# A hybrid encoder layer: weight loads, value splits, output projection and mixture in a new order

## The chip, the cores and the metric

The kernel runs on one core of a Trainium2 chip. The metric is the device time of one execution in microseconds; for the kernel before it is the median of three runs. The engines are TensorE (PE), VectorE (DVE), ScalarE (ACT), GpSimd (POOL) and SyncE (SP, which issues DMAs).

## The reference, cut to what matters

Both batches (1024 tokens, "a"; 512 tokens, "b") go through the same layer with the same weights, in f32:

```python
h = rms_norm(x, pre_w)
cols = jnp.einsum('bsd,dc->bsc', h, w_in)          # 1024 -> q|k, v, o, z, gates, attention q,k,v, z, merge gates
y_m = mlstm_mixer(...) * silu(m_z)                 # 4 heads x 256, both directions, chunks of 128
y_a = dilated_attention(a_qkv, rel_table) * silu(a_z)   # 3 groups x 8 heads x 64, mixed by softmax denominators
merged = g[:, :, 0] * (y_m @ w_pm) + g[:, :, 1] * (y_a @ w_pa)
out = merged @ w_out
return x + rms_norm(out, post_w)
```

## The kernel before, in words

**Precision.** Nearly every product is three matmuls: each operand is split into a rounded high part (ACT copy) and the rest as a low part (DVE or POOL subtraction), and `mm3` (L174 to L179) adds high x high, high x low and low x high. A split must be ready before the product's first matmul (L177) and its low part before the second or third.

**Part one** (to about 1030 us) projects batch a with a Strassen-like scheme: 7 products instead of 8 for a 2x2 block form. `combos` makes the seven combinations of the input, H. `value_group` (L347) makes the value columns in 4 groups; a group has 7 products (m1, m2, m6, m7, m5, m4, m3), each of 4 token tiles x 4 k x 3 = 48 matmuls of 322 columns. Its splits (L362 ACT, L363 DVE) use two buffers (vhi and vlo, `bufs=2`) in turn, in the order in which they are traced: m1's, then s2 (for m6), then w12 (for m2), and so on. PSUM has 8 banks, and a product takes 4. Evictions are DVE adds (such as L409 and L436), high/low splits into vz (L387, L388; three buffers) and stores (L389, L392). Each group loads its weights (va, vb) and makes sums of them on POOL (L343 to L345, vsum). `lanes` is a chain of small gate computations on ACT and DVE with a few PE transposes; its steps are advanced one by one between the products of groups 1 and 2. Then 38 calls of `unit_pair` (L439) make the other columns, two units of 128 columns at a time: two loads (L445), splits (L453, L454), POOL sums, 7 products of 12 matmuls of 512 columns.

In part one PE's order is the program's. The orders of ACT, DVE, POOL and SP are chosen when the kernel is compiled, by a scheduler that prefers what stands earlier in the program among what it takes to be ready; `high_priority` puts an instruction ahead of others. On the chip each engine then works strictly in its order.

**Part two** (from about 1030 us) runs the mLSTM of a, the attention of a, the mLSTM of b, the attention of b and the rest, in rounds (`mlstm` L788, `attend` L1142). In every round `fill` puts in dense work: a list of units (projections of batch b, then for each block of 512 tokens the two branch projections w_pm and w_pa and the output projection w_out), cut into steps of 3 matmuls of 512 columns or 6 of 256. `STEPS` (L1410) sets how many steps fall into each stage. Here the orders of PE and SP are both the program's.

`Fill.load` (L124) and `load_w` (L221) bring the weights: `load_w` issues the DMA into one of two raw buffers (L229) and traces the split (L230 ACT, L231 DVE) into one of three ring buffers, five after the third stage. `ready` counts the weights split, `taken` those in use, `base` the first still held; `ahead` is how many may be split ahead (2, later 3).

`final` (L1359) is the output projection of a block: for each half u of the columns it takes four weights at once and runs 4 token tiles t one after the other, 8 k-steps of three matmuls each, in one of two PSUM banks. A tile is closed by a square with a sum (L1388 ACT), and, for the first half, a product with the post-norm weights (L1390 DVE), for the second the norm (L1394 to L1397), the residual from tile xo (loaded at L1384, two buffers) and the sum (L1400); the result is stored at the next tick (L193) or, for the last tile, at once (L1404).

`combine` (L1201) mixes the three dilation groups of a token tile: `load(t+1)`, `mix(t)` (some 15 DVE instructions, L1219 to L1239), a yield, `turn(t-1)` (PE transposes L1244, DVE product L1246), a yield. The mixture of a runs beside the rounds of the mLSTM of b, one step a round; that of b beside the last fill steps. `split` (L1272) then fetches the rows (tile ymr, L1281) for the branch projections.

`tick` (L195) issues stores that have come due and some of the queued loads (L214); `spread` (L205) sets how many a tick, so that the loads for the next attention unit are spread over the rounds of the present one; `need` issues what is still queued.

Of the kernel before, what the change touches and what calls it, by code (L numbers as in the profile page):

```python
# [112 lines left out]
class Fill:  # L113
# [3 lines left out]
    def __init__(self, net, units):  # L117
        self.net, self.units, self.gen = net, list(units), None
        self.srcs = [x for u in self.units for x in u.srcs]
        self.ready, self.taken, self.base, self.ahead = [], 0, 0, 2  # L120
        self.rate = self.due = 0.0
        self.done = 0

    def load(self):  # L124
        while len(self.ready) < min(self.base + len(self.net.wsplit), self.taken + self.ahead, len(self.srcs)):
            self.ready.append(self.net.load_w(*self.srcs[len(self.ready)]))

    def weights(self, first=True):

        if first:  # L130
            self.base = self.taken
        self.taken += 1
        self.load()
        return self.ready[self.taken - 1]

# [25 lines left out]
class Net:  # L161
# [59 lines left out]
    def load_w(self, src, kt=KT, cols=P):  # L221

        nc = self.nc
        n = kt * cols
        raw = self.wraw.pop(0)
        hi, lo = self.wsplit.pop(0)
        self.wraw.append(raw)
        self.wsplit.append((hi, lo))
        nc.sync.dma_start(raw[:, :n], src)  # L229
# [117 lines left out]
    def value_group(self, g, T, H, sb, us, co, ps):  # L347

        nc = self.nc
        N = 4 * VW  # L350
        wa = sb.tile([P, 2, N], F32, name="va", bufs=1)
# [7 lines left out]
        def split(x):  # L359
            hi = sb.tile([P, N], F32R, name="vhi", bufs=2)  # L360
            lo = sb.tile([P, N], F32R, name="vlo", bufs=2)
            nc.scalar.activation(hi, x, AF.Copy)  # L362
            nc.vector.tensor_sub(lo, x, hi.bitcast(F32))  # L363
# [11 lines left out]
        def out(t, blk, jc, c):  # L375
# [7 lines left out]
            if a0 < a1:  # L383
# [5 lines left out]
                nc.sync.dma_start(T.vs[:, r, a0 - 16:a1 - 16].rearrange("a t c -> t a c"), z[:, :, :w].bitcast(F32))  # L389
            a0 = max(lo, 16 + D)  # L390
            if a0 < hi:
                nc.sync.dma_start(T.av[r, a0 - 16 - D:hi - 16 - D], c[:, a0 - c0:])  # L392
# [3 lines left out]
        m1 = product(B11, split(wa[:, 0]))  # L396
# [31 lines left out]
        yield  # L428
        m4 = product(T4, split(wb[:, 1]))
# [4 lines left out]
        m3 = product(B22, split(s[:, 1]))  # L434
        for t in range(4):
# [3 lines left out]
    def unit_pair(self, ua, ub, H, sb, cp, ps):  # L439

        nc = self.nc
        ws = []
        for u in (ua, ub):
            w = sb.tile([P, 2, BLK], F32, name="pw_raw", bufs=4)
            last = nc.sync.dma_start(w, self.a["w_in"][u].rearrange("p (a c) -> p a c", a=2))  # L445
            ws.append(w)
        wa, wb = ws

        def split(x):
            n = x.shape[1]  # L450
            hl = sb.tile([P, 2, 2, BLK], F32R, name="phl", bufs=4)
            hi, lo = hl[:, 0], hl[:, 1]
            nc.scalar.activation(hi[:, :n], x, AF.Copy)  # L453
            nc.vector.tensor_sub(lo[:, :n], x, hi[:, :n].bitcast(F32))  # L454
            return [(hi[:, i].rearrange("p (k c) -> p k c", c=P), lo[:, i].rearrange("p (k c) -> p k c", c=P))
                    for i in range(n)]
# [7 lines left out]
        a11, a12 = split(wa)  # L464
        s = sb.tile([P, 2, BLK], F32, name="psum_w", bufs=2)
        self.sums(wa, wb, s)
        s1, s2 = split(s)
        nc.gpsimd.tensor_sub(s[:, 1], wa[:, 1], s[:, 1])
        s3, a22 = split(wb)
# [3 lines left out]
        u2 = sb.tile([P, BLK], F32, name="pu2", bufs=2)  # L473
# [6 lines left out]
        u3 = sb.tile([P, BLK], F32, name="pu3", bufs=1)  # L480
# [6 lines left out]
        s4, = split(s[:, 1:2])  # L487
        m3 = product(B22, s4)
        nc.vector.tensor_add(q[0][1], u2, m3)
        return c, last  # L490
# [651 lines left out]
    def attend(self, T, fill, steps, first, banks, outs, after=None, beside=None, at=()):  # L1142
# [5 lines left out]
        with ExitStack() as st:  # L1148
# [52 lines left out]
    def combine(self, T, bank, cs, ys, sb):  # L1201
# [50 lines left out]
        for t in range(T.n):  # L1252
# [33 lines left out]
    def along(self, units, make, every):  # L1286
# [3 lines left out]
        def wrap(u, last):  # L1290
            def go(weights):
# [7 lines left out]
                if last:  # L1299
                    for _ in got["g"]:  # L1300
                        pass
# [57 lines left out]
    def final(self, T, b):  # L1359
# [4 lines left out]
        def make(weights):  # L1364
# [6 lines left out]
            for u in range(2):  # L1371
                c = slice(u * BLK, (u + 1) * BLK)
                w = [[x.rearrange("p (k c) -> p k c", c=BLK) for x in weights(kp == 0)] for kp in range(4)]
                for t in range(4):
                    r0 = b * BLK + t * P
                    ts = slice(t * P, (t + 1) * P)
                    p = self.ps_d.tile([P, BLK], F32, name="dense")
                    for k in range(KT):
                        wk = w[k // 2]
                        hi, lo = m[k // 4]  # L1380
                        self.mm3(p, (hi[:, k % 4, ts], lo[:, k % 4, ts]), (wk[0][:, k % 2], wk[1][:, k % 2]), k == 0, k == KT - 1)
                        if k == 3 and u == 1:
                            xt = xo[t] = sb.tile([P, D], F32, name="xo", bufs=2)
                            nc.sync.dma_start(xt, T.x[r0:r0 + P])  # L1384
                        if k < KT - 1:
                            yield
                    jk = sb.tile([P, BLK], F32, name="mg", bufs=2)
                    nc.scalar.activation(jk, p, AF.Square, accum_out=ss[:, t, u:u + 1])  # L1388
                    if u == 0:
                        nc.vector.tensor_mul(o[:, t], p, pw[:, c])  # L1390
# [250 lines left out]
```

## Time and profile before

| what | value |
|---|---|
| runs of the kernel before | 2473.7, 2474.91, 2484.87 us; median 2474.91 |
| the profiled execution | 2470.32 us, of which the span from the first to the last instruction is 2468.4 |
| mean granted TensorE clock | 0.969 |
| DVE, ACT, POOL busy | 1515.6, 1126.4, 742.9 us |
| DMA | 419.86 MB, 170 GB/s on the mean |

A busy PE is one with at least one matmul in flight. Idle time before an instruction is put down to what released it. The granted clock is 1 or 0.5 at any moment; a mean below 1 over a stretch says what part of it ran at half speed.

### The profile page before, as it was taken

What the parts mean: (1) busy time and instruction counts of PE and PEld (TensorE: products, weight loads), DVE (VectorE), ACT (ScalarE), POOL (GpSimd) and SP (SyncE); (2) the same over time, 40 slices, a digit from 0 to 9 for tenths busy, and PEclk for the clock granted to TensorE, in tenths of its full rate; (3) what the DMA queues carried; (4) which work ended last, traced back from release to release, by engine and by line L of the source; (5) the groups of instructions that cost most, each with busy time, mean ns of one, the idle gap of its engine ahead of it and who ended that gap; (6) DMA issues with size and microseconds to landing.
All of it is one profiled execution on the core that took longest, in us unless ns stands there. A gap on an engine that the chain in (4) does not pass through costs nothing. (4 is left out here: it accounts for less than half of the span.)

```text
span 2468.4 us, 36244 instructions
## 1 busy us (share of the span) xinstructions
PE 2300.6 (93%) x12486; PEld 1994.0 (81%) x12486; DVE 1515.6 (61%) x2957; ACT 1126.4 (46%) x2389; POOL 742.9 (30%) x924
## 2 busy tenths in 40 slices
PE   4989899999999999999999999989988989989878
PEld 4888888888888888798998798978877878777766
DVE  7664467679986555467777554545698534445464
ACT  5331134444444333366765465556555444434322
POOL 5212133243332233145555200010355231324022
PEclk8999999999999999999999999999999989999999
DMA  3342244553222242555567678875776575585653
GB/s 146 106 113 88 101 185 184 197 188 118 102 100 89 94 145 103 195 201 194 167 213 208 173 210 226 223 199 168 220 226 200 169 249 183 181 249 177 205 182 127
DMA packets 251582, 419.86 MB, mean 170 GB/s; under 512 B 24872, under 2 KB 149992, under 8 KB 251400
## 3 DMA queue, kind: packets, MB, share of 16 engines
q1 hardware_dynamic: 247944, 404.98, 51.8%
q10 hardware_dynamic: 3456, 12.58, 1.3%
q8 instruction: 99, 1.62, 0.3%
q14 instruction: 83, 0.68, 0.1%
HBM read 297.48 MB, written 128.39 MB: 173 GB/s over the span
## 5 line engine op out<-in xcount | busy, mean ns | idle before, releaser
L177 PE MATMUL d<-Hh,phl 128*128 128x512 f32 x1064 | 415.3, 390 | 7.2 <-ACT phl L453 7.2
L179 PE MATMUL d<-Hh,phl 128*128 128x512 f32 x1064 | 415.5, 390 | 1.8 <-DVE phl L454 1.8
L178 PE MATMUL d<-Hl,phl 128*128 128x512 f32 x1064 | 415.0, 390 | 0.0
L231 DVE TENSOR_TENSOR wl<-wraw,wh 128x1024 fp32r<-128x1024 f32 x130 | 166.2, 1279 | 203.7 <-ACT wh L230 203.2
L177 PE MATMUL dense<-H,wh 128*128 128x512 f32 x672 | 281.1, 418 | 10.8 <-ACT wh L230 6.2
L179 PE MATMUL dense<-H,wl 128*128 128x512 f32 x672 | 267.6, 398 | 0.0
L178 PE MATMUL dense<-H,wh 128*128 128x512 f32 x672 | 267.6, 398 | 0.0
L177 PEld LDWEIGHTS d<-Hh,phl 128*128 128x128 f32 x1064 | 200.4, 188 | 49.1 <-ACT phl L453 7.5
L179 PEld LDWEIGHTS d<-Hh,phl 128*128 128x128 f32 x1064 | 200.4, 188 | 45.5 <-DVE phl L454 4.2
L178 PEld LDWEIGHTS d<-Hl,phl 128*128 128x128 f32 x1064 | 200.4, 188 | 41.7
L230 ACT ACTIVATE wh<-wraw 128x1024 fp32r<-128x1024 f32 x130 | 137.6, 1058 | 192.5 <-DMA wraw<-w_in 76.0
L1113 ACT ACTIVATE ls<-ls,nm 128x256 f32<-128x256 f32 (+1 forms) x288 | 129.9, 452 | 106.7 <-DVE nm L1111 89.6
L453 ACT ACTIVATE phl<-pw_raw 128x1024 fp32r<-128x1024 f32 x76 | 80.5, 1060 | 170.9 <-PE d L179 120.9
L179 PEld LDWEIGHTS dense<-H,wl 128*128 128x128 f32 x672 | 128.8, 192 | 30.8 <-DVE wl L231 1.4
L177 PEld LDWEIGHTS dense<-H,wh 128*128 128x128 f32 x672 | 129.4, 193 | 27.5 <-ACT wh L230 6.6
L178 PE MATMUL d<-vlo,Hh 128*128 128x322 f32 x448 | 144.3, 322 | 7.7 <-DVE vlo L363 7.7
L177 PE MATMUL d<-vhi,Hh 128*128 128x322 f32 x448 | 145.4, 325 | 6.4 <-ACT vhi L362 6.4
L453 ACT ACTIVATE phl<-psum_w 128x1024 fp32r<-128x1024 f32 x76 | 64.3, 846 | 190.6 <-PE d L179 153.7
L1109 DVE CUSTOM_DVE_ANT_0 ls<-lg,bias 128x256 f32<-128x256 f32 (+1 forms) x288 | 93.2, 360 | 91.3 <-PE lg L1097 40.7
L343 POOL TENSOR_TENSOR psum_w<-pw_raw 128x512 f32<-128x512 f32 x38 | 60.5, 1592 | 279.5 <-DMA pw_raw<-w_in 260.6
L179 PE MATMUL d<-vhi,Hl 128*128 128x322 f32 x448 | 143.4, 320 | 0.0
L178 PEld LDWEIGHTS dense<-H,wh 128*128 128x128 f32 x672 | 129.5, 193 | 15.6
(497 smaller groups left out, 5805.7 us busy)
## 6 DMA issues: line engine op xcount, KB each, us to landing
pw_raw<-w_in SPq DMA_DIRECT2D x76, 512.0 KB
wraw<-w_in SPq DMA_DIRECT2D x76, 512.0 KB
aqk_a<-pwk SPq DMA_DIRECT2D x48, 512.0 KB
aqk_b<-sw SPq DMA_DIRECT2D x48, 256.0 KB
wraw<-w_pm SPq DMA_DIRECT2D x24, 512.0 KB
wraw<-w_out SPq DMA_DIRECT2D x24, 512.0 KB
wraw<-w_v SPq DMA_DIRECT2D x18, 512.0 KB
erep<-erow SPq DMA_DIRECT2D x16, 512.0 KB
```

Source lines behind the costliest of these rows:

```text
L177: nc.tensor.matmul(out, lh, rh, start=start, stop=False)
L178: nc.tensor.matmul(out, lh, rl, start=False, stop=False)
L179: nc.tensor.matmul(out, ll, rh, start=False, stop=stop)
L230: self.splits = (nc.scalar.activation(hi[:, :n], raw[:, :n], AF.Copy), nc.vector.tensor_sub(lo[:, :n], raw[:, :n], hi[:, :n].bitcast(F32)))
L231: nc.vector.tensor_sub(lo[:, :n], raw[:, :n], hi[:, :n].bitcast(F32)))
L343: nc.gpsimd.tensor_add(s[:, 0], wb[:, 0], wb[:, 1])
L453: nc.scalar.activation(hi[:, :n], x, AF.Copy)
L1109: nc.vector.tensor_tensor_reduce(out=ls[:, hh], in0=ts["lg"][hh], in1=bt[:, hh], scale=1.0, scalar=NEG, op0=OP.add, op1=OP.max, accum_out= ...
L1113: nc.scalar.activation(ls[:, hh], ls[:, hh], AF.Exp, bias=nm[:, hh:hh + 1], accum_out=ot[:, 128 + hh:129 + hh])
```

## The change

Seven edits, in the order of the program:

1. **Weights of fill units.** The load and the split are parted (`fetch`, `split_w`). Each time a weight is split, the load of the one after it is issued too.
2. **Value groups.** The first split's buffers are taken ahead of the group's loads; splits are traced with high priority; w12 is split before s2; the last product's evictions come after a yield of their own; `lanes` advances at every second step.
3. **Start of the pairs.** The last value group is stopped before its last evictions; the value tiles are given back; the first pair's loads and its first two splits are traced; only then come the evictions (behind the second split on DVE) and eight stores (`late`, behind the loads on SP). The tiles u move to the other side of SBUF, so that the pair's tiles lie over the value weights.
4. **Pairs.** Loads and splits of every pair have high priority; the four split buffers become two kinds of two.
5. **Both attentions.** All loads for unit 1 are issued in the first round after they are queued.
6. **Output projection.** Two token tiles overlap: slot by slot, k-steps 4 to 7 of one tile alternate with k-steps 0 to 3 of the next, two at a time, and after each pair of k-steps of a half's last tile `release` gives a weight's buffer back and loads on.
7. **Mixture.** Three steps a tile instead of two, with the transposes two yields after the mixture of the next tile; the last attention has 300 fill steps instead of 330, and the mixture of b 86 instead of 50.

The core of the diff:

```diff
     def load(self):
         while len(self.ready) < min(self.base + len(self.net.wsplit), self.taken + self.ahead, len(self.srcs)):
-            self.ready.append(self.net.load_w(*self.srcs[len(self.ready)]))
+            self.fetch(len(self.ready) + 1)
+            self.ready.append(self.net.split_w(*self.raws[len(self.ready)]))
+            self.fetch(len(self.ready) + 1)
+
+    def fetch(self, n):
+        while len(self.raws) < min(n, len(self.srcs)):
+            self.raws.append(self.net.load_w(*self.srcs[len(self.raws)]))
...
+    def release(self):
+        self.base += 1
+        self.load()
...
     def load_w(self, src, kt=KT, cols=P):
         raw = self.wraw.pop(0)
+        self.wraw.append(raw)
+        self.nc.sync.dma_start(raw[:, :kt * cols], src)
+        return raw, kt * cols
+
+    def split_w(self, raw, n):
         hi, lo = self.wsplit.pop(0)
...
-        def split(x):
-            hi = sb.tile([P, N], F32R, name="vhi", bufs=2)
-            lo = sb.tile([P, N], F32R, name="vlo", bufs=2)
-            nc.scalar.activation(hi, x, AF.Copy)
-            nc.vector.tensor_sub(lo, x, hi.bitcast(F32))
+        def split(x, at=None):
+            hi, lo = at or place()
+            with self.tc.high_priority():
+                nc.scalar.activation(hi, x, AF.Copy)
+                nc.vector.tensor_sub(lo, x, hi.bitcast(F32))
...
+        w12 = split(wa[:, 1])
         s2 = split(s[:, 1])
-        w12 = split(wa[:, 1])
...
+        if late is not None:
+            store = lambda *x: late.append(x)
         m4 = product(T4, split(wb[:, 1]))
...
         m3 = product(B22, split(s[:, 1]))
+        yield
         for t in range(4):
...
+    def pair_split(self, x, hl):
+        n = x.shape[1]
+        hi, lo = hl[:, 0], hl[:, 1]
+        with self.tc.high_priority():
+            self.nc.scalar.activation(hi[:, :n], x, AF.Copy)
+            self.split_end = self.nc.vector.tensor_sub(lo[:, :n], x, hi[:, :n].bitcast(F32))
...
+    def pair_weights(self, ua, ub, sb):
...
+            with self.tc.high_priority():
+                last = self.nc.sync.dma_start(w, self.a["w_in"][u].rearrange("p (a c) -> p a c", a=2))
...
-                            self.spread(T.n - 1)
+                            self.spread(T.n - 1 if i else 1)
...
                 mix(t)
             yield
+            yield
             if t > 0:
                 turn(t - 1, az[t - 1])
             yield
+        yield
         yield
         turn(T.n - 1, az[T.n - 1])
...
+            w, p = {}, {}
+            for slot in range(2 * 8 + 2):
+                for i in (slot // 2 - 1, slot // 2):
+                    u, t = divmod(i, 4)
+                    if not 0 <= i < 8:
+                        continue
+                    kp = slot - 2 * i
+                    if t == 0:
+                        w[u, kp] = [x.rearrange("p (k c) -> p k c", c=BLK) for x in weights(u == kp == 0)]
+                    if kp == 0:
+                        p[i] = self.ps_d.tile([P, BLK], F32, name="dense")
...
+                    for k in (2 * kp, 2 * kp + 1):
...
+                        if k == KT - 1:
+                            close(u, t, c, p.pop(i))
+                        if t == 3 and k % 2 == 1:
+                            weights.__self__.release()
...
-STEPS = (310, 232, 194, 330, 50)
+STEPS = (310, 232, 194, 300, 86)
...
-                        for _ in values[g]:
-                            next(lanes, None)
+                        for j, _ in enumerate(values[g]):
+                            if j % 2 == 0:
+                                next(lanes, None)
...
-                for _ in values[3]:
-                    pass
-            with ExitStack() as s2:
-                sb = N.pool(s2, "pairs", 1, "left")
+                for _ in range(7):
+                    next(values[3])
+            with ExitStack() as s4:
+                sb = N.pool(s4, "pairs", 1, "left")
+                coming = N.pair_weights(U_AQ, U_AQ + 1, sb)
+                with tc.issue_after(N.split_end.ins):
+                    for _ in values[3]:
+                        pass
+                for x in late:
+                    with tc.issue_after(coming[1].ins):
+                        nc.sync.dma_start(*x)
+                s2.close()
...
-            fill.ahead = 3
+            fill.ahead = 4
...
-                fill.stage(STEPS[4], 2 * B.n + 4)
+                fill.stage(STEPS[4], 3 * B.n + 6)
```

More of the change, by code (lines that the diff above doesn't have):

```diff
@@ L119, in __init__ @@
         self.srcs = [x for u in self.units for x in u.srcs]
-        self.ready, self.taken, self.base, self.ahead = [], 0, 0, 2
+        self.raws, self.ready, self.taken, self.base, self.ahead = [], [], 0, 0, 2
         self.rate = self.due = 0.0
@@ L345, in sums, with value_group @@
         nc.gpsimd.tensor_sub(wb[:, 0], wa[:, 0], wb[:, 0])
-    def value_group(self, g, T, H, sb, us, co, ps):
+    def value_group(self, g, T, H, sb, us, co, ps, late=None):
         nc = self.nc
+        store = nc.sync.dma_start
         N = 4 * VW
+        place = lambda: [sb.tile([P, N], F32R, name=x, bufs=2) for x in ("vhi", "vlo")]
+        first = place()
         wa = sb.tile([P, 2, N], F32, name="va", bufs=1)
@@ L462, in product @@
             return p
[L464 to L467, printed above, removed]
         nc.gpsimd.tensor_sub(s[:, 1], wa[:, 1], s[:, 1])
-        s3, a22 = split(wb)
+        s3, a22 = split(wb, places[0])
         c = [cp.tile([P, 2 + 2 * BLK], F32, name="c") for _ in range(2)]
@@ L486, in unit_pair @@
         nc.vector.tensor_add(q[1][0], u3, m4)
-        s4, = split(s[:, 1:2])
+        s4, = split(s[:, 1:2], places[1])
         m3 = product(B22, s4)
         nc.vector.tensor_add(q[0][1], u2, m3)
-        return c, last
+        return c
     def conv_unit(self, u, T, raw, w):
@@ L1385, in make @@
[L1385 to L1390, printed above, removed]
-                        yield
-                        continue
-                    o1 = sb.tile([P, BLK], F32, name="mg", bufs=2)
-                    nc.vector.tensor_add(ss[:, t, 4:5], ss[:, t, 0:1], ss[:, t, 1:2])
@@ L1445, in co @@
                     return opened[0]
-                values = [N.value_group(g, A, H, vw, us, co, ps) for g in range(4)]
+                values = [N.value_group(g, A, H, vw, us, co, ps, late if g == 3 else None) for g in range(4)]
                 N.small(N.const)
```

105 lines of the change are left out of this document (55 added, 50 removed).

## The prediction

> **What bounds the kernel now.** I read the page first. TensorE (PE) is busy for 2300.6 of 2468.4 us; no other engine passes 61%. What can be won is PE's idle time (167.8 us) and the time in which PE ran at a reduced clock.
>
> ```profile
> span 2468.4 us, 36244 instructions
> ...
> PE 2300.6 (93%) x12486; PEld 1994.0 (81%) x12486; DVE 1515.6 (61%) x2957; ACT 1126.4 (46%) x2389; POOL 742.9 (30%) x924
> ...
> PE   4989899999999999999999999989988989989878
> PEclk8999999999999999999999999999999989999999
> ```
>
> The last row is the clock in tenths: the slices under 9 lie where PE's row dips. Next I read the waits of PE (what waited, for whom: us, times, longest).
>
> ```profile
> PE dense L177 <- ACT wh L230: 14.0, 3, 6.8
> PE lg L1097 <- DMA V1a<-aqk_b: 8.9, 2, 7.3
> PE d L178 <- DVE vlo L363: 7.7, 5, 2.6
> PE d L177 <- ACT phl L453: 7.2, 1, 7.2
> PE tp L1244 <- DVE Q L1239: 6.9, 1, 6.9
> PE a L1244 <- DVE wd L1226: 6.5, 1, 6.5
> PE d L177 <- ACT vhi L362: 6.4, 5, 1.9
> ```
>
> Each of these lines is a place that the change edits. Last, I took the busy times of the stretches around them (start:end, length, PE, PEld, DVE, ACT, POOL, PEclk, DMA share, GB/s).
>
> ```profile
> 107.86:132.69 24.83, 18.52 (x98) 17.71 (x98) 13.21 (x19) 8.42 (x19) 3.07 (x1) 0.79 0.54 161
> 174.43:196.77 22.34, 17.44 (x96) 16.72 (x97) 10.16 (x15) 5.93 (x12) 3.10 (x1) 0.85 0.59 156
> 196.77:221.60 24.83, 24.83 (x170) 24.83 (x169) 14.07 (x22) 5.13 (x4) 0.33 (x1) 1.00 0.28 90
> 232.52:252.55 20.03, 17.22 (x99) 15.89 (x99) 5.55 (x7) 4.21 (x6) 2.96 (x1) 0.91 0.10 35
> 288.29:305.00 16.71, 9.47 (x29) 7.11 (x29) 5.14 (x4) 3.72 (x5) 9.13 (x6) 0.69 0.49 166
> 1800.00:1850.00 50.00, 40.43 (x215) 34.14 (x214) 46.19 (x133) 27.87 (x64) 23.93 (x43) 0.93 0.73 222
> 1995.00:2020.00 25.00, 16.07 (x72) 13.14 (x72) 9.00 (x16) 11.78 (x24) 9.56 (x10) 0.73 0.92 281
> 2345.00:2400.00 55.00, 41.27 (x167) 31.93 (x167) 34.39 (x76) 11.99 (x16) 11.16 (x9) 0.91 0.57 183
> ```
>
> A stall costs twice: PE idles, and then runs slow. With length W, a stretch loses at least idle/2 + (1-PEclk)W (all idle lay in slow time) and at most idle + (1-PEclk)W; I use the middle.
>
> **Value groups.** The third row is undisturbed: 170 matmuls in 24.83 us, 0.146 us each, so the 96 of two products need 14.0. The other three such rows take 24.83, 22.34 and 20.03: lost 10.8 + 8.3 + 6.0 = 25.1 us. The cause is an order. Splits use two buffers in turn; after the first product's split the old code splits s2, not yet needed, into the second, so w12 must wait until the first product has freed the first: in the ACT timeline it starts at 119.40, when that product ended at 118.80. With w12 first, the split (ACT 1.28 + DVE 1.50) lies beside a product of 7.1 us, and s2 beside the next. Ahead of evictions, the group's first split starts when its buffer is free (100.7), not at 107.17. Late next are the evictions: up to 2.8 us later, but a bank is wanted only two products (14 us) on. POOL's sums run beside some splits, where one took 3.09 instead of 1.50; 7.1 covers that. I take 22, ends 0 and 25. The gate lanes, advanced at every second step, have 14 us instead of 7 for their vector chain: the stretch 132.69 to 174.43 has 2.9 us idle and PEclk 0.96, lost 4.6 at most; I take 4, ends 0 and 4.6.
>
> [...]
>
> **Pair start.** The first pair's loads are issued at 289.59, when the value pools have closed; PE waits 7.24 us: lost 8.8 to 12.4. Now the loads overlay value tiles read before (the weights va by 244, vb by 270), the splits lie in the last product (7.1 us), and the last evictions and eight stores come after (DVE holds those four adds behind the second split; their banks are wanted four pair products, 11 us, later). What is late next is the first c tile, which reuses the old u tiles: their stores must land by the third product, 8 us on; eight issues of 0.45 us and some 3 us of landing fit. I take 9.5, ends 0 and 12.4.
>
> **Loads a unit ahead.** ACT no longer sits before a split on a load in flight (76 us before L230 alone); that matters where PE waits. After an output projection SyncE is held by stores:
>
> ```profile
> 2174.19 1.00 SPq L1404 DMA_DIRECT2D y_prompt<-xo  x2
> 2176.24 7.42 SPq L229 DMA_DIRECT2D wraw<-w_pm  x3
> ```
>
> The next weights are queued behind those stores, and PE idles 6.2 (2170 to 2190, PEclk 0.83: lost 6.5 to 9.6) and 6.8 (2320 to 2345, 0.80: 8.4 to 11.8), middle 18.1. Each release now loads as the last token tile passes, ahead of these stores. I take 14, ends 0 and 21. At 1032 to 1050 (idle 2.1, PEclk 0.91: lost 2.7 to 3.7) I take 2, ends 0 and 3.7. No load is added; each raw buffer's earlier split is already done when its load is issued.
>
> **Staggered tiles.** The same 24 x 24 matmuls. A PSUM bank is wanted again 12 matmuls after its tile (2.8 us), not 24 (5.6). The last tile ended at 2461.87 and its second read at 2463.45: 1.6. Beside attention the cover is 3.4 (4 of some 7 steps of a round of 5.9 us) and the reads took 1.7 (2134.16 to 2135.82). It fits, but a weight split in front (1.06 or 1.23) uses up the slack; one collision of 0.5 in every sixth of 24 tiles is 2 us: -2, ends 0 and -12.
>
> **First load of the second attention.** Fourteen loads were spread over three rounds behind ymr fetches on SP; the last V1a was issued at 2003.66 and landed 5.9 later, the first at 1991.61. At 0.5 each from there, the last goes at 1998.1 and lands at 2004, 5.5 earlier than 2009.5: of 8.93 idle some 3.4 stays. Lost is 11.2 to 15.7; I take 7, ends 0 and 15.7. In the first attention the same burst delays weight loads, which now have a unit's time (12 us): 0, ends -3 and 1.
>
> **Mixture in three steps, and the step counts.** For the long batch (1750 to 1900; idle 5.5 + 9.6 + 8.1, PEclk 0.97, 0.93, 0.93) 20 to 32 us are lost, with DVE at 46.19 of 50. Its transposes wait 12.4 us for it (rows L1244). Five rounds instead of three lie between a mixture and its transpose, and it spreads over 28 rounds instead of 19, into a stretch (1900 to 1950) with DVE at 33.91. Only those waits are meant, and crowding may return: 10, ends -5 and 20. For the short batch 86 instead of 50 steps, at 0.7 us, cover it: 60 us instead of 35, for a stretch that idles 13.73. There DVE splits waited for w_pa in front of the mixture's adds: the early load helps too. Lost 11.8 to 18.7; I take 10, ends 0 and 18.7. The 30 steps taken from attention shorten a round from 6.9 to 6.25 steps; its waits on SP may grow, counted below.
>
> **Unseen collisions.** Every order on ACT and DVE shifts. The nearest rows are single waits of 1 to 3 us, each with a slow 3.4 us (1.7 lost): I take four, -12, ends 0 and -40.
>
> **Sum.** 22 + 4 + 9.5 + 14 + 2 - 2 + 7 + 0 + 10 + 10 - 12 = 64.5. The profiled execution took 2470.3 us (its span 2468.4): 2405.8. The median of the runs, 2474.9, stands 4.6 above; the forecast is 2410 us.
>
> **Rivals.**
> 1. Half is given back, 2443. Behind the stalls stand engines that are nearly full (DVE 46.19 of 50) and a DMA share of 0.92 at 281 GB/s, so a wait that goes comes back as the next. Against: the value, pair and release terms have slack around them. Half of 64.5 is 32. Chance 0.22.
> 2. It does not do what it says, 2469: the compiled order keeps splits behind evictions, and SP, blocked by ymr, is as late as before; only the swap of s2 and w12 stays (single waits 1.9, 1.9 and 1.7 us, 6 in all). Chance 0.05.
> 3. Slower, 2520. One mechanism: in the 38 pairs (288 to 1025 us, about 2 us lost today) splits go ahead of evictions, and DVE is near full in the eight conv pairs (45.04 of 50 from 600 to 650). If a bank comes free late by one DVE split (1.23) and PE slows (1.7), a pair costs 2.9 us: 110 in all. From 22 pairs on it eats the 64.5. Against it: eight banks for seven products, and DVE at 34 of 50 in the attention pairs. Chance 0.09.
>
> The forecast holds 0.64: 2385 to 2430. Range: its terms at their upper ends give 122 without a collision, 2353; that all come full is unlikely, so I go to 2374, and up to 2456 to hold the first rival. A measurement of this kernel tells about 0.5% (12 us) from no change: faster 0.86, same 0.05, slower 0.09.
>
> **What would show it.** Right: no PE wait on vhi or vlo between 100 and 260; PE back to back across the first pair; w_pm issued ahead of the last y store; L1244 gone from the waits; V1a's wait under 4 us; PEclk at 1.00 in the value stage. Wrong: PE waits before the pairs' first matmuls; waits of dense on L1388 or L1390 (stagger); lg or o waits in the second attention growing with the shorter rounds.

## The result, and the profile after

The changed kernel takes 2373.36 us (median of four runs, 2370.15 to 2381.38); the kernel before, run beside it, 2479.89 us. The ratio is 0.9575, with a 95% interval from 0.9536 to 0.9614: 4.25% less time, about 105 us. The profiled execution took 2373.65 us, with a span of 2371.4 us, 97.0 us shorter than the profiled span before, where the sum of the prediction was 64.5 us. The mean granted clock went from 0.969 to 0.984.

The page of the kernel after, its span, busy times, PE's row and the clock's row (tenths, 40 slices):

```profile
span 2371.4 us, 36316 instructions
...
PE 2266.9 (96%) x12486; PEld 1975.3 (83%) x12486; DVE 1498.1 (63%) x2957; ACT 1130.4 (48%) x2389; POOL 738.3 (31%) x924
...
PE   5999999999999999999999999999969999999998
...
PEclk7999999999999999999999999999989999999999
```

PE still has its 12486 matmuls, is busy 33.7 us less and idle 63.3 us less (104.5 instead of 167.8). Behind the start, the clock row has one dip left, in slice 30 (1719 to 1778 us), where PE's row dips too. The waits of PE after name its cause (what waited, for whom: us, times, longest):

```profile
PE a L855 <- DMA Q<-qk_b: 14.7, 2, 10.1
...
PE lg L1129 <- DMA V0a<-aqk_b: 5.4, 1, 5.4
...
PE d L190 <- DVE vlo L382: 3.6, 3, 1.3
...
PE lg L1129 <- DMA V1a<-aqk_b: 2.8, 1, 2.8
PE dense L189 <- DVE o L1411: 2.8, 3, 1.1
PE dense L189 <- ACT wh L245: 2.7, 1, 2.7
```

Of the seven lines shown of before, the waits on phl (pair start) and on the mixture's transposes (L1244, now L1276) are gone; wh went from 14.0 to 2.7, vlo from 7.7 to 3.6, V1a from 8.9 to 2.8, and vhi from 6.4 to 0.8. At the top stands a wait that was not there: Q, 14.7 us.

The stretches of the kernel after, in the columns of the prediction (start:end, length, PE, PEld, DVE, ACT, POOL, PEclk, DMA share, GB/s): the value groups, the start of the pairs, and the place of the new wait.

```profile
100.00:150.00 50.00, 46.92 (x298) 45.61 (x297) 33.59 (x68) 20.84 (x38) 6.29 (x3) 0.97 0.58 143
150.00:200.00 50.00, 48.66 (x323) 47.91 (x322) 31.55 (x49) 14.00 (x25) 11.82 (x4) 1.00 0.43 108
200.00:266.20 66.20, 66.20 (x437) 65.16 (x436) 32.80 (x48) 14.04 (x14) 20.19 (x9) 1.00 0.30 103
266.00:292.00 26.00, 26.00 (x117) 21.56 (x116) 16.01 (x19) 8.74 (x12) 11.47 (x10) 1.00 0.46 162
...
1750.00:1800.00 50.00, 34.14 (x190) 29.85 (x191) 37.05 (x92) 24.86 (x55) 18.97 (x33) 0.83 0.58 186
```

PE is busy from 200 us into the pairs without a break (66.20 of 66.20, 26.00 of 26.00), at full clock, across the point where it had waited 7.24 us. The last row shows the opposite: 15.9 us idle in 50, clock 0.83.

Where the 97.0 us came from, by stages. A stage begins with its first matmul; the value groups and the pairs end with the end of their last one:

| stage | before, us | after, us | difference |
|---|---|---|---|
| start to the second value product | 63.7 | 61.8 | -1.9 |
| value groups | 224.6 | 204.4 | -20.2 |
| gap before the pairs, and the pairs | 737.1 | 726.6 | -10.5 |
| pairs to the first fill step | 6.8 | 6.2 | -0.5 |
| mLSTM of a | 361.8 | 354.9 | -6.9 |
| attention of a, and on to the mLSTM of b | 352.3 | 327.5 | -24.8 |
| mLSTM of b | 230.3 | 230.7 | +0.5 |
| attention of b to the end | 491.8 | 459.3 | -32.5 |

The attention of b and the rest stand together because 30 fill steps moved from one to the other. Where the text below gives the attention of a or of b alone, it runs from its first matmul to the start of its last product of queries and keys (lg).

### The profile page after: what moved, and what is told of

Read it like the earlier page. It is cut to its first block, busy times and chain, and to the rows that moved or that the text cites. A ratio compares the mean times of both kernels' runs of the same rounds, so it can differ in the third digit from the quotient of the medians.

```text
span 2371.4 us, 36316 instructions
## 1 busy us (share of the span) xinstructions
PE 2266.9 (96%) x12486; PEld 1975.3 (83%) x12486; DVE 1498.1 (63%) x2957; ACT 1130.4 (48%) x2389; POOL 738.3 (31%) x924
## 5 line engine op out<-in xcount | busy, mean ns | idle before, releaser
L189 PE MATMUL dense<-H,wh 128*128 128x512 f32 x672 | 276.9, 412 | 4.5 <-ACT wh L245 2.7
L190 PE MATMUL dense<-H,wh 128*128 128x512 f32 x672 | 264.3, 393 | 0.0
L191 PE MATMUL d<-Hh,phla 128*128 128x512 f32 x608 | 237.0, 390 | 1.8 <-DVE phla L466 1.8
L189 PE MATMUL d<-Hh,phla 128*128 128x512 f32 x608 | 236.6, 389 | 0.0
L190 PE MATMUL d<-Hl,phla 128*128 128x512 f32 x608 | 236.5, 389 | 0.0
L246 DVE TENSOR_TENSOR wl<-wraw,wh 128x1024 fp32r<-128x1024 f32 x130 | 163.2, 1256 | 99.8 <-ACT wh L245 99.3
L245 ACT ACTIVATE wh<-wraw 128x1024 fp32r<-128x1024 f32 x130 | 137.0, 1054 | 105.5 <-PE dense L190 46.0
L191 PE MATMUL d<-Hh,phlb 128*128 128x512 f32 x456 | 177.4, 389 | 0.0
L189 PE MATMUL d<-Hh,phlb 128*128 128x512 f32 x456 | 177.4, 389 | 0.0
L190 PE MATMUL d<-Hl,phlb 128*128 128x512 f32 x456 | 177.4, 389 | 0.0
L191 PEld LDWEIGHTS d<-Hh,phla 128*128 128x128 f32 x608 | 114.1, 188 | 27.1 <-DVE phla L466 3.5
L190 PEld LDWEIGHTS d<-Hl,phla 128*128 128x128 f32 x608 | 114.1, 188 | 23.7
```

The source lines that it names most:

```text
L189: nc.tensor.matmul(out, lh, rh, start=start, stop=False)
L190: nc.tensor.matmul(out, lh, rl, start=False, stop=False)
L191: nc.tensor.matmul(out, ll, rh, start=False, stop=stop)
L245: self.splits = (nc.scalar.activation(hi[:, :n], raw[:, :n], AF.Copy), nc.vector.tensor_sub(lo[:, :n], raw[:, :n], hi[:, :n].bitcast(F32)))
L246: nc.vector.tensor_sub(lo[:, :n], raw[:, :n], hi[:, :n].bitcast(F32)))
```

## The experiments

Each ran beside the kernel before on the same chip. Ratios are to that kernel; spans are of the profiled executions, and stages have the bounds of the table. "After" is the changed kernel. Edit 4 (priority in the pairs) and the step of `ahead` from 3 to 4 were not run alone.

### The weight loads, taken out and put in alone

The largest surprise was the attention of a: 24 us where the prediction had a term of nothing. Two runs: after without the early load, and before with only the early load.

```diff
# no_ahead: the kernel after without the second fetch
             self.ready.append(self.net.split_w(*self.raws[len(self.ready)]))
-            self.fetch(len(self.ready) + 1)
```

> The changed kernel, but each weight's load is issued only with its own split (one line taken out of Fill.load). Theory: ScalarE's splits waiting for loads in flight are what held the first attention up (339.1 us before, 315.3 after, although its PE work is the same). Then the first attention goes back to 330 to 340 us, ACT L245 again waits for wraw loads by over 60 us, and the kernel takes about 2395 to 2405. Rival (the first attention was shortened by the burst of loads for unit 1, not by the early weight loads): first attention stays at 315 to 320, total within 8 us of the changed kernel.

Measured: 2423.53 us, ratio 0.9769 [0.9732, 0.9805], 50 us over after, more than the 22 to 32 expected. The attention of a is back at 342.6 us (315.3 after, 339.1 before), the mLSTM of a at 367.2 (354.9 after).

```diff
# before_ahead: the kernel before with the load and the split parted
-            self.ready.append(self.net.load_w(*self.srcs[len(self.ready)]))
+            self.fetch(len(self.ready) + 1)
+            self.ready.append(self.net.split_w(*self.raws[len(self.ready)]))
+            self.fetch(len(self.ready) + 1)
...
```

> The kernel before, with only the weight loads issued a unit ahead of their splits. Theory (this part alone frees the first attention, and part of the waits after the output projections): first attention 315 to 322 us instead of 339, total 2440 to 2452. Rival (it needs the other parts): first attention 335 or more, total within 8 us of before.

Measured: 2409.58 us, ratio 0.9716 [0.9686, 0.9747]; the span is 60.4 us shorter than before, and the kernel is 30 us faster than the best expected. The attention of a takes 314.2 us, all that after has there; the stages behind it gain too (mLSTM of b 226.3, attention of b to the end 472.3).

So this one edit is worth 50 us on top of the others and 60 to 70 alone. Why, the waits of ACT in the attention of a show (wh is the high part of a weight, pts and ot belong to the softmax and the output of the attention). First the kernel before:

```profile
ACT wh L230 <- DMA wraw<-w_in: 44.9, 16, 5.5
ACT ls L1113 <- DVE nm L1111: 37.4, 32, 2.9
ACT wh L230 <- DMA wraw<-w_v: 16.2, 4, 5.8
```

Then the kernel after:

```profile
ACT ls L1145 <- DVE nm L1143: 40.0, 31, 2.0
ACT ot L1166 <- PE o L1164: 26.1, 33, 2.8
ACT pts L1155 <- PE pt L1152: 13.6, 21, 1.1
ACT wh L245 <- PE dense L190: 9.7, 5, 5.1
ACT wh L245 <- DMA wraw<-w_v: 4.7, 1, 4.7
```

And no_ahead:

```profile
ACT wh L244 <- DMA wraw<-w_in: 51.4, 19, 5.5
ACT ls L1144 <- DVE nm L1142: 38.1, 31, 4.2
ACT wh L244 <- DMA wraw<-w_v: 17.7, 5, 5.6
```

ACT sat 61.1 us before splits whose load was in flight, 69.1 us without the early load, and 4.7 us with it. PE hardly waits for those splits (two are traced ahead). It waits for what stands behind them on ACT and DVE. One place in the timelines of the kernel before shows the chain (start, us, engine and line, operation, out<-in, and in brackets the idle time before and what ended it). SP issues the load:

```profile
1524.31 0.58 SPq L229 DMA_DIRECT2D wraw<-w_v  x1
```

ACT, in the same timeline of before, stands still for it:

```profile
1531.05 1.06 ACT L230 ACTIVATE wh<-wraw 128x1024 fp32r<-128x1024 f32 x1 [5.81 <-DMA wraw<-w_v]
1532.01 0.26 ACT L1134 ACTIVATE ot<-o 128x128 f32<-128x128 f32 x1
1532.17 0.71 ACT L522 ACTIVATE sraw<-sraw,hnw 128x512 f32<-128x512 f32 x1
1532.78 0.59 ACT L1123 ACTIVATE pts<-pt 128x512 f32<-128x512 f32 x1
```

DVE, of the same kernel, has its own half of the split in its order:

```profile
1532.13 1.23 DVE L231 TENSOR_TENSOR wl<-wraw,wh 128x1024 fp32r<-128x1024 f32 x1 [5.39 <-ACT wh L230]
```

And PE, of the same kernel, waits for the copy that came late:

```profile
1533.42 0.78 PE L1132 MATMUL o<-K,pts 128*128 128x64 f32 x5 [2.48 <-ACT pts L1123]
```

ACT idles 5.81 us until the load has landed; the softmax copy pts comes three instructions behind the split, and PE waits 2.48 us for it. The trace puts that wait down to pts, not to wh. DVE idles 5.39 us too. no_ahead has the same place at 1507.49 (5.56 us of ACT, 2.21 us of PE). In that stage PE was idle 18.6 us before, 22.9 in no_ahead and 4.7 after. The place stands for most of it: of the 18.6 us, 13.2 lie in nine waits that ended within 4 us of the start of an ACT split that had waited for its load, in no_ahead 15.4 of the 22.9, in after 0.5 of the 4.7. With the idle time went slow time: 17.1 us of the stage at half clock before, none after. The 13.9 us of idle time and half of the 17.1 make 22.4 of the 23.8 us that the stage gained.

### The value groups: the order of two splits

```diff
# before_swap: the kernel before with the two lines swapped, and nothing else
-        s2 = split(s[:, 1])
         w12 = split(wa[:, 1])
+        s2 = split(s[:, 1])
```

> The kernel before with two lines swapped: w12 is split ahead of s2, without any priority. Theory (the order of the two splits in a two-buffer rotation is the structural cause of the value stage's stalls): the value stage from the second product to the last goes from 224.6 to 208 to 213 us, total -12 to -16 us. Rival (the evictions standing ahead of the splits are the cause): value stage 219 us or more, total -5 us at most.

Measured: 2463.5 us, ratio 0.9926 [0.99, 0.9952], a gain of under 1%; the value stage takes 208.6 us instead of 224.6, 16.0 less. Of this the attention of a gave 6 us back (345.1 instead of 339.1).

```diff
# no_swap: the kernel after with the old order
-        w12 = split(wa[:, 1])
         s2 = split(s[:, 1])
+        w12 = split(wa[:, 1])
```

> The changed kernel with s2 split ahead of w12 again; splits keep their priority over evictions. Theory (order of the buffers is the cause; swapping alone brought 16 of 20.2 us to the kernel before): the value stage goes from 204.4 back to 216 to 222 us, PE waits for vhi at the start of every m2, total +12 to +18. Rival (priority alone is enough): value stage under 208, total within 4.

Measured: 2392.52 us, ratio 0.9637 [0.9615, 0.966], 19 us over after; the value stage 221.0 us, 16.6 over after. The waits of PE in this run's value groups:

```profile
PE d L190 <- DVE vlo L382: 8.7, 5, 3.0
PE d L189 <- ACT vhi L381: 5.4, 4, 2.0
```

High priority, the buffers taken first and the spaced lanes are all in this run, and vhi and vlo wait as before (6.4 and 7.7). The order of the two splits is the cause of 16 of the 20.2 us; the rest of edit 2 is worth some 4 us (208.6 against 204.4), and its parts were not run alone.

### The output projection

```diff
# old_final: the kernel after with the output projection of before, tile after tile, no release
-            for slot in range(2 * 8 + 2):
-                for i in (slot // 2 - 1, slot // 2):
...
-                        if t == 3 and k % 2 == 1:
-                            weights.__self__.release()
+            for u in range(2):
+                w = [[x.rearrange("p (k c) -> p k c", c=BLK) for x in weights(kp == 0)] for kp in range(4)]
+                for t in range(4):
...
```

> The changed kernel with the output projection as before: four weights taken at once, token tiles one after the other, no release; weight loads still one unit ahead. Theory (release lets the next unit's splits go ahead of the last stores): after each of the first two output projections PE waits 2 to 7 us for wh again, and from the second attention to the end the kernel takes 459 + 8 to 16 us. Rival (the early loads alone had removed these waits): within 3 us of 459. Second rival (halved PSUM slack costs more than release brings): faster than the changed kernel by over 3 us.

Measured: 2396.29 us, ratio 0.9655 [0.9634, 0.9675], 23 us over after. From 2040 us on, the waits of PE in it:

```profile
PE dense L189 <- ACT X L245: 6.9, 1, 6.9
PE lg L189 <- DVE ot L1141: 5.6, 1, 5.6
PE tp L1276 <- DVE Q L1271: 4.0, 1, 4.0
PE dense L189 <- ACT wh L245: 3.0, 1, 3.0
```

Waits for the split of the next weights (L245) come back although loads run a unit ahead: 6.9 us inside the second projection, for the w_out of its second half (ended at 2234.60), and 3.0 us behind it, for w_pm (2272.02), but none behind the first, where the theory had one too. By the code, the ring has no free buffer before a half of the projection ends. The attention of b to the end takes 480.4 us instead of 459.3, more than the 8 to 16 us expected. This run takes out the release and the overlap of tiles together, so it does not price them apart. That after releases while it computes shows on SP (kernel after):

```profile
2104.43 1.00 SPq L205 DMA_DIRECT2D y_prompt<-xo  x2
...
2109.71 0.33 SPq L237 DMA_DIRECT2D wraw<-w_pm  x1
2110.75 1.00 SPq L1425 DMA_DIRECT2D y_prompt<-xo  x2
```

A load of w_pm goes out ahead of the last y store, as the prediction asked; before, it stood 2 us behind it and was then issued over 7.42 us.

### The burst of loads

```diff
# no_burst: the kernel after with the loads of unit 1 spread again
-                            self.spread(T.n - 1 if i else 1)
+                            self.spread(T.n - 1)
```

> The changed kernel with the loads for attention unit 1 spread over T.n-1 rounds again. Theory (the burst matters only at the start of the second attention): PE's wait for V1a there grows from 2.8 to 7 to 9 us with slow clock, total +5 to +9 us; first attention unchanged at 315 us. Rival (the burst shortened the first attention): first attention 330 or more. Second rival (the early weight loads alone removed the wait): total within 2 us.

Measured: 2370.43 us, ratio 0.9564 [0.9532, 0.9597], the same as after. The first wait of the attention of b is there again, in no_burst:

```profile
PE lg L1129 <- DMA V1a<-aqk_b: 11.5, 2, 7.9
```

Yet the stage takes 280.2 us against 283.6 after. What the burst saves at V1a (11.5 to 2.8) it partly pays at once, in 5.4 us for V0a of the next unit, and the rest of the stage gives back what is left. The theory held for the wait and not for the time: the burst is worth nothing that shows.

### The long batch's mixture and the new wait for Q

```diff
# mix2: two steps for the long batch, three for the short one
-            yield
+            if T.n == 4:
+                yield
...
```

> The changed kernel with the long batch's mixture in two steps a tile again (the short batch's stays at three). Theory (three steps took away the transposes' waits, L1276, and let PE run into a wait for Q<-qk_b of 14.7 us instead, so the stage from the mLSTM of b to the second attention stayed at 230 us): the stage stays within 4 us of 230.7; L1276 waits of 6 to 12 us come back and the Q wait shrinks below 8. Rival (three steps are worth the 10 us that I forecast): stage 238 or more.

Measured: 2367.22 us, ratio 0.9547 [0.952, 0.9574]. The mLSTM of b takes 224.5 us, less than with three steps (230.7) and than before (230.3), and less than the theory allowed. The difference is clear of noise in the stage: five traces with the early load and the three steps as in after (after, no_burst, no_swap, old_final, short_old) take 228.9 to 232.6 us there and wait 14.2 to 15.2 us for Q. In mix2 the Q wait is gone, and a wait for the mixture stands at the top of that stage:

```profile
PE a L1276 <- DVE K L1271: 8.2, 2, 6.2
```

Why did three steps bring the wait for Q? SP of the kernel after around it:

```profile
1757.88 0.32 SPq L205 DMA_DIRECT2D qk_b<-sw  x1
1758.29 1.36 SPq L226 DMA_DIRECT2D Q<-qk_b  x3
...
1760.17 0.43 SPq L205 DMA_DIRECT2D ym_a<-K  x1
1766.35 0.37 SPq L226 DMA_DIRECT2D K<-az_a  x1
...
1769.65 0.47 SPq L226 DMA_DIRECT2D Q<-qk_b  x1
```

The waits of SP from 1740 to 1778 in the same kernel name what held it:

```profile
SPq L205 <- DVE r L950: 14.7, 1, 14.7
SPq L226 <- DMA ym_a<-K: 5.7, 1, 5.7
```

SP is idle up to 1757.88 before a store (of the unit that holds q and k) whose data DVE has not finished, and again until 1766.35, since the load of the next mixture's K must wait until the store from K has landed; the last Q load is behind both, and PE waits 4.65 and 10.06 us, ending at 1764.41 and 1775.24. Two theories: the fill unit that makes q and k of b comes just in time, so any delay reaches Q; or the transposes, now late after the mixture, let the K store run into the K load. Three runs:

```diff
# conv_early: eight more fill steps ahead of the stage
-STEPS = (310, 232, 194, 300, 86)
+STEPS = (310, 240, 186, 300, 86)
```

> The changed kernel with 8 fill steps (one unit) moved from the mLSTM of b into the first attention: STEPS 310, 240, 186. Theory (the 14.7 us wait for Q<-qk_b is a chain from a unit that the fill computes just in time: convolution, store, load): the wait falls below 6 us and the stage from the mLSTM of b to the second attention is 8 to 16 us shorter, of which 5.6 are the moved steps, which the first attention gains (315 to 321); total -4 to -12. Rival (SyncE, held by the mixture's loads, sets the wait, not the unit): the wait stays over 10 us and the total within 3.

Measured: 2388.1 us, ratio 0.9624 [0.9602, 0.9645], 15 us slower than after. The wait stays:

```profile
PE a L855 <- DMA Q<-qk_b: 15.3, 4, 8.7
```

The first theory, as I had put it, falls: with the unit earlier in steps the wait is as long, and the stage grows to 240.0 us. The rival's total (within 3 us) missed too: the attention of a takes 9.5 us more for the 5.6 of moved steps. Why, no run tells.

```diff
# turn1: the long batch's transposes one yield after the mixture 
-            yield
-            yield
-            if t > 0:
-                turn(t - 1, az[t - 1])
-            yield
+            for j in range(3):
+                if t > 0 and j == (2 if T.n == 4 else 1):
+                    turn(t - 1, az[t - 1])
+                yield
```

> The changed kernel; for the long batch the transposes of the last token tile come one yield after the mixture of the next instead of two (still three steps a tile, 28 rounds), so the store of the mixed tile comes due before the next tile's load into the same buffer. Theory (SyncE, in order, waits 5.7 us for that store's landing in front of the last Q load, and PE waits for Q): SyncE's wait for ym_a<-K shrinks below 3 us, PE's wait for Q<-qk_b falls from 14.7 to under 6, the stage from the mLSTM of b to the second attention takes 218 to 224 us instead of 230.7, total -6 to -12. Rival (the unit computed just in time sets the wait): the Q wait stays at 12 or more, total within 3.

Measured: 2365.48 us, ratio 0.9568 [0.9547, 0.9589]. The wait in turn1:

```profile
PE a L855 <- DMA Q<-qk_b: 7.4, 3, 6.2
```

```diff
# turn0: the transposes of the tile before at once behind the mixture (against turn1)
-                if t > 0 and j == (2 if T.n == 4 else 1):
+                if t > 0 and j == (2 if T.n == 4 else 0):
```

> As the run before, but the transposes come directly after the next tile's mixture, three rounds after their own mixture, as far as in the kernel before; the store then comes due a round ahead of the load. Theory: SyncE's wait for ym_a<-K under 1.5 us, Q wait under 4 us, and the waits of the transposes L1276 for DVE stay below 8 us because the mixture is spread over 28 rounds; stage 216 to 222 us. Rival (the distance of three rounds is too short, as in the kernel before): L1276 waits of 12 us or more, stage 226 or more.

Measured: 2366.53 us, ratio 0.9571 [0.9552, 0.959]; the Q wait is 9.5 us. Both place the K store earlier, and SP's wait for its landing ahead of the last Q load falls from 5.7 us to 0.7 (turn1) and to nothing (turn0). The Q wait falls by 7.3 and 5.2 us and the stage to 226 us (226.3 and 225.8), less than expected in both runs; the totals can't be told from after's. The second theory holds for about half of the wait. The other half stands behind the store ahead of the Q loads: SP still waits 13.3 us (turn1) and 12.2 us (turn0) for its DVE data, against 14.7 in after, and 3.2 us at most for such stores around that place in mix2. Why DVE is later there with three steps, no run tells.

### The short batch's mixture, and the best version

```diff
# short_old: two steps for the short batch, and the step counts of before
-            yield
+            if T.n == 8:
+                yield
...
-STEPS = (310, 232, 194, 300, 86)
+STEPS = (310, 232, 194, 330, 50)
...
-                fill.stage(STEPS[4], 3 * B.n + 6)
+                fill.stage(STEPS[4], 2 * B.n + 4)
```

> The changed kernel with the short batch's mixture in two steps and the step counts 330 and 50 again; the long batch keeps three. Theory (60 us of cover instead of 35 took away the waits of its transposes; early weight loads alone did not, as the kernel before with early loads alone still waited 16 us there): L1276 waits of 8 to 16 us come back in the last 130 us, from the second attention to the end +8 to +16 us. Rival (the early loads and the release together suffice): within 3 us.

Measured: 2378.36 us, ratio 0.9617 [0.9597, 0.9638]; 5 us over after, with intervals that overlap. The attention of b to the end takes 465.7 us, 6.4 more than after; seven other traces with the short batch's mixture and the output projection as in after (no_ahead left out) take 454.3 to 459.7 there. Waits of 6.0 us on L1276 come back, below the 8 to 16 expected: right in sign, too small in size.

```diff
# mix2_spread: mix2 and no_burst together
-                            self.spread(T.n - 1 if i else 1)
+                            self.spread(T.n - 1)
...
-            yield
+            if T.n == 4:
+                yield
...
```

> The changed kernel without the two edits that brought nothing: the long batch's mixture in two steps a tile and the loads of attention unit 1 spread over T.n-1 rounds. Theory (three steps for the long batch and the burst are neutral to harmful): ratio to the kernel before 0.950 to 0.957, 2358 to 2372 us, the stage from the mLSTM of b to the second attention 222 to 227. Rival (the burst was neutral only because the Q wait delayed what follows; without that wait V1a's wait counts): 2373 to 2382 us, V1a's wait 8 us or more and the second attention 285 or longer.

Measured: 2365.99 us (median of five runs), ratio 0.9527 [0.9513, 0.954], the lowest of all. The stage takes 223.8 us, as expected. V1a's wait is back at 12.0 us, as the rival had it, but the attention of b takes no longer for it (282.5 us against 283.6 after). It drops the two parts that brought nothing and is 0.5% under after, at the edge of what can be told (after's interval begins at 0.9536). It makes the kernel before 4.7% faster.

## Why the prediction was right or wrong

The sign was right. The size was not: 2373.4 us lies at the very lower end of the range of 2374 to 2456 (0.6 us under it, less than its runs differ), and the gain was half as large again as forecast (97.0 against 64.5 us of span). By its own steps:

| step | forecast, us | measured, us |
|---|---|---|
| value groups and lanes | 22 + 4 | 20.2 (the swap alone 16.0) |
| pair start | 9.5 | 10.5 (gap and pairs together) |
| loads ahead | 14 + 2 | 50 (taken out of after) to 70 (put into before) |
| output projection | in the 14, and -2 | 23 (old form in after) |
| first load of the second attention | 7 | 0 |
| long batch's mixture | 10 | 0 against before, -6 against two steps beside the other edits |
| short batch's mixture, step counts | 10 | 5 to 6 (old form in after) |
| collisions | -12 | Q: 14.7 of idle time |

By the stages of the table above the miss has one place. The mLSTM and the attention of a gained 31.7 us, where the sum had 2; that is 29.7 of the 32.5 us by which the gain passed the forecast. That the other terms add up to nearly what they should is partly luck: the value groups gave 6 us less, the mLSTM of b gave nothing instead of 10, and the 12 set aside for collisions covered most of that.

**Loads ahead: the step that failed.** The prediction had the 76 us before L230 in hand and set most of them aside with "that matters where PE waits", by which it meant waits of PE for wh. It counted two releases and one stall near 1040 us. The runs showed that a split in ACT's order holds what is behind it (5.81 us up to 1531.05 before, with a softmax copy behind it), and that PE's waits for those carry other names (pts and ot of the attention, sraw of a fill unit). In the attention of a those single waits were 0.2 to 4.7 us, spread over 339 us, and the prediction gave that stage a term of nothing, for the burst. The edit's rows on the page say it too: ACT's idle time before the split fell from 192.5 to 105.5 us, and DVE's from 203.7 to 99.8. These are the rows of the kernel before (line, engine, form, count, busy, mean ns, idle before and its releaser):

```profile
L231 DVE TENSOR_TENSOR wl<-wraw,wh 128x1024 fp32r<-128x1024 f32 x130 | 166.2, 1279 | 203.7 <-ACT wh L230 203.2
...
L230 ACT ACTIVATE wh<-wraw 128x1024 fp32r<-128x1024 f32 x130 | 137.6, 1058 | 192.5 <-DMA wraw<-w_in 76.0
```

And of the kernel after:

```profile
L246 DVE TENSOR_TENSOR wl<-wraw,wh 128x1024 fp32r<-128x1024 f32 x130 | 163.2, 1256 | 99.8 <-ACT wh L245 99.3
L245 ACT ACTIVATE wh<-wraw 128x1024 fp32r<-128x1024 f32 x130 | 137.0, 1054 | 105.5 <-PE dense L190 46.0
```

**Output projection.** The mechanism was right, and the size of the release too low: 23 us against 12 (14 - 2). With the loads a unit ahead but no buffer to split into, waits of 6.9 and 3.0 us on L245 return in and behind the second projection; the releases are what lets the early load act there. The two edits overlap, so 50 and 23 must not be added. What shows of the stagger's price is the waits on L1411 and L1418, 2.8 and 1.2 us, where the forecast had 2.

**Value groups.** Right in the mechanism and nearly in size. What stays, 3.6 us on vlo, is three waits of at most 1.3 us; from 170 us on the stage has no wait on vhi or vlo. Here the clock can be weighed: PE's idle time in the stage fell from 17.0 us (224.6 less 207.64 busy) to 4.4 (204.4 less 199.98), by 12.5 us of the 20.2; the other 7.7 us are busy time at a higher clock, with 26.5 us of the stage at half clock before and 4.1 after (2.6 and 0.7 of them the end of a stretch that began ahead of the stage). The longest single wait there was 2.6 us before and 1.3 after, so with waits as short as these the stage still lost more than their idle time, as the prediction's sum had it.

**Pair start.** Right: no wait on phl, PE at 26.00 of 26.00.

**First load of the second attention.** The local half came as forecast (V1a under 4 us). That the time would follow was wrong: the term priced one wait and not the one that the same loads have a unit later (V0a, 5.4 us).

**Long batch's mixture.** The waits on the transposes went, and one of equal size took their place through SP, an engine whose order the step had not followed: a store that waits for DVE and a load that waits for a landing, with Q behind them. The allowance for collisions covered it in amount and named no place.

**Rivals.** The first, half given back, happened in two terms (burst, long mixture) and nowhere else. The second fell: every part but those two does what it says, and the swap alone, which it priced at 6 us, brought 16.0 in its stage. The third, slower pairs, fell: from their first matmul to their last, the pairs went from 729.9 to 726.7 us.

## What to carry to other kernels

A wait of an engine that works in order isn't priced by who waits for its result, but by all that stands behind it in that order (here ACT's 5.81 us before a split became PE's 2.48 us on pts): take the instructions that follow a DMA wait on ACT or DVE, and look for PE's waits on those. With two buffers in turn, the order in which tiles are asked for can matter more than priority: here 16 us against some 4 for priority and the rest of that edit. When a wait on one engine is moved, follow the queue that issues the DMAs through the same stretch, since a store that waits for its data holds the loads behind it: here one held SP for 14.7 us, with the loads of Q behind it.

## What the runs showed of the hardware

**The clock.** The traces of before and after have only two clocks, 1 and 0.5, and half clock comes in stretches of 3.41 us and its multiples (6.83, 10.24, 13.65, 17.07) apart from the last one, cut by the kernel's end: 25 stretches with 152.7 us before, 10 with 76.6 after. The starts show the same length: within each of the two traces they lie whole multiples of 3.4133 us apart, to 0.005 us (117.06 and 1001.12 in the kernel after are 884.05 us apart, 259 times 3.4133).

A wait of 2.48 us that ended at 1533.42 in the kernel before was followed by half clock from 1534.05, for 3.41 us, as the prediction's allowance of one slow stretch a wait had it. But the length of one wait does not tell: of the twelve single waits of 0.9 to 1.5 us in the kernel after, behind the first product, one was followed by half clock within a microsecond (it ended at 116.69; the slow stretch begins at 117.06), and a wait of 3.14 us that ended at 2255.60 by none. What goes with the clock in these two traces is PE's busy share of a piece of 3.4133 us, when the traces are cut into such pieces in step with the starts of the slow stretches. From the first clock record on (21.94 us before, 21.49 after) they have 1338 such pieces at full clock. All 23 with PE busy under 40% were followed by half clock, and none of the 1290 with 60% or more; of the 25 between, 12 were. Of 65 pieces at half clock, all 26 with PE busy under 70% were followed by another, 6 of the 7 up to 90%, and none of the 32 with 90% or more. In the 3.41 us ahead of 117.06 PE was busy 1.90, or 56%: ahead of the wait of 1.12 us that ended at 116.69 lies one of 0.39. The wait of 3.14 us lies across two pieces, with PE busy 61% and 48%. This is read off the traces; no run varied it by itself.

**A load in flight.** Two weight loads of 512 KB, issued among others on SP, took 6.7 and 6.5 us from issue to the split that waited for them (1524.31 to 1531.05 before, 1501.02 to 1507.49 in no_ahead). A unit has 8 steps, and the attention of a holds 232 steps in 339 us, so a unit takes some 12 us there. These loads took about half of that, so by this estimate one that goes out a unit ahead has landed when its split comes up. Of 61.1 us of such waits before, 4.7 stayed in after.
